# Gathering expert rows of x2 over its norm, with scale and shift applied behind the transposes, low parts on VectorE and an earlier routing of tiles 3 to 5

## The chip, the cores and the metric

The kernel runs on one core of a Trainium2 chip. The metric is the device time of one execution in microseconds, as the median of several runs. The profile is of one further execution. Its engines are TensorE (PE in the rows, with PEld for its weight loads), VectorE (DVE), ScalarE (ACT), GpSimd (POOL) and SyncE (SP), which issues most DMAs; an issue row has the engine's name with a q behind it.

## The reference

One layer with 1024 tokens of 1024 columns, and 256 context tokens. A mixer of gated linear attention and 2-D pooling ends in an output projection and a gated residual; behind it stands a mixture of 32 experts, two for each token. Cut to the part that the change touches:

```
x  = x + gt_a * (concat(o, pooled) @ w_out)                 # x2 in the kernel
h2 = rmsnorm(x, norm2_g) * (1 + sc_m) + sh_m                # norm2_g, sc_m, sh_m: one value a column
pg = softmax(h2 @ w_rg);  group = top 1 of 4
le = softmax of the 8 logits (h2 @ w_re) of that group;  experts = top 2
x  = x + gt_m * sum over the two experts of weight * (silu(a) * u) @ w_e_out,   a, u = h2 @ w_e_in
return rmsnorm(x, final_norm_g)
```

All arithmetic is f32. TensorE's products of f32 data are made of three passes with a high part (`hh`, `woh`) and a low part (`hl`, `wol`), the rest of a value less its high part. The products of the experts are done in one pass of f32.

## The kernel before, in words

**The mixer** (about 0 to 428 us) works on eight tiles of 128 tokens. A stretch at about 305 us opens its last part: `router_cols` transposes the 24 x 128 tile `rows` (shift, scale and gain of the second norm, for the router's weights `wr`), `pool_mix` makes 16 products of the pooled channels (L900), their evictions on ScalarE give the pooled half of `mix`, and the loop over the tiles (`n`, called the qp loop below) computes scores, masks them into `am`, and projects the first 512 columns of the output. Its loads go out on SyncE; `csl` is a table of constants for the routing. At `n == 6` the qp loop loads `shm` and `scm`, the shift and scale as rows of 1024 columns on all partitions, and VectorE multiplies the second norm's gain, loaded in two pieces `n2b`, into `scm` (L1056). This part ends at 428.

**The out1 loop** (428 to 495 us) makes the other 512 columns for the eight tiles, in an order that is written by hand for TensorE and VectorE; the other engines' order follows from it. A tile has 24 products of 128 x 512, three for each of eight pieces of the inner dimension, `tokproj(..., range(3))` and `range(3, 8)`. For a tile: `out_proj` makes the high part on ScalarE and the low part on GpSimd (L889; on VectorE for tile 0), `out1_x2` adds the residual in two operations on VectorE (L1302, L1303) and ScalarE sums the squares, `out1_rstd` gives `rst`, one over the norm, `logit1` transposes x2 for the router and `logit1_mm` multiplies it, `out1_bias` and an operation behind the logit products (L1334) give the logits `lga`. `out1_h2` makes the rows that the experts read: x2 times `rst` times `scm` on VectorE (L1323), plus `shm` on GpSimd (L1324), for tile 7 on ScalarE and GpSimd (L1320, L1321). The row goes to `h_d` in DRAM.

**The routing** works on three groups of tiles, A (0 to 2), B (3 to 5) and C (6, 7). For each group `route(a, b)` is a generator with three stages and a rest, all on VectorE: stage 1 chooses the expert group (L1111 to L1130, where L1099 repeats a small operation for each tile), stages 2 and 3 the two experts (to `ohb`, L1150), the rest their weights. Then TensorE counts tokens for each expert (`counts`, L1187), `place` gives each token its place, and `tables` adds up lists of tokens on TensorE (L1238, L1247). `idx`, the list for the gather, needs all three groups.

**The experts** (519 to about 784 us) run in blocks of up to 128 gathered tokens. GpSimd gathers rows of `h_d` into `hall`; `Block.rows` transposes a block in two halves of four transposes (L1644), ScalarE evicts the first half (L1650), VectorE the second (L1648), and the products with the experts' weights follow. Weights are loaded ahead into every slab of SBUF that has become free.

Of the kernel before, what the change touches and what calls it, by code (L numbers as in the profile page):

```python
# [14 lines left out]
OP = mybir.AluOpType  # L15
# [119 lines left out]
def hybrid_layer(ctx, tc, x, c, ctx_in, c_ctx, w_ada, b_ada, norm1_g, w_in, w_decay, b_decay, gla_norm_g,  # L135
# [44 lines left out]
    ones_r = early.tile([P, 32], F32, name="ones_r")  # L180
    ccol = early.tile([P, 8], F32, name="ccol")
# [670 lines left out]
    gta, shm, scm = hslab[0:3]  # L852
# [39 lines left out]
    with tc.tile_pool(name="qp", bufs=2) as qp:  # L892
        wbs = qp.tile([P, 36], F32, name="wbs", bufs=1)
        onef = qp.tile([P, P], F32, name="onef", bufs=1)
        gp.memset(onef, 1.0)

# [8 lines left out]
        def router_cols():  # L905

            pt = bank(6, 4, 5)
            te.transpose(pt[:, 0:24], rows, ident[:24, :24])
            col = qp.tile([P, 24], F32, name="col", bufs=1)
            ve.tensor_copy(col, pt[:, 0:24])  # L910
            ve.scalar_tensor_tensor(col[:, 8:16], col[:, 8:16], 1.0, col[:, 16:24], op0=OP.add, op1=OP.mult)
# [119 lines left out]
        with tc.manual_schedule(engines={mybir.EngineType.PE}):  # L1031
# [7 lines left out]
            for n in range(NT + 6):  # L1039
# [9 lines left out]
                if n == 6:  # L1049
                    sc.dma_start(shm, row_bcast(mod_d[D:2 * D], D))  # L1050
                    sc.dma_start(scm, row_bcast(mod_d[2 * D:3 * D], D))
                    for b in range(2):
                        ns = slice(b * 512, (b + 1) * 512)
                        n2b = qp.tile([P, 512], F32, name="xr")
                        sc.dma_start(n2b, row_bcast(norm2_g[0, ns], 512))
                        ve.scalar_tensor_tensor(scm[:, ns], scm[:, ns], 1.0, n2b, op0=OP.add, op1=OP.mult)  # L1056
# [235 lines left out]
    def out1_in(i):  # L1292
# [4 lines left out]
        po1[i], h1[i] = out_proj(i, wo2)  # L1297
# [17 lines left out]
    def out1_h2(i):  # L1315
        h2 = x2b[i % 3]
        for src, b in ((h2[:, 0:512], 0), (x1[i], 1)):
            dst, bs = h2[:, b * 512:(b + 1) * 512], slice(b * 512, (b + 1) * 512)
            if i == NT - 1:
                sc.activation(dst, src, AF.Copy, scale=rst[:, i:i + 1])  # L1320
                gp.tensor_tensor(dst, dst, scm[:, bs], OP.mult)  # L1321
            else:
                ve.scalar_tensor_tensor(dst, src, rst[:, i:i + 1], scm[:, bs], op0=OP.mult, op1=OP.mult)  # L1323
            gp.tensor_tensor(dst, dst, shm[:, bs], OP.add)  # L1324
        sy.dma_start(h2_d[i * P:(i + 1) * P], h2)
# [10 lines left out]
    with tc.manual_schedule(engines={mybir.EngineType.PE, mybir.EngineType.DVE}):  # L1336
        out1_in(0)
        for f in wo2_steps:
            f()
        rA, rB, rC = route(0, 3), route(3, 6), route(6, 8)  # L1340
        for n in range(NT):
            if n + 1 < NT:
                out1_in(n + 1)
            tokproj(po1[n], h1[n], wo2, range(3))
            if n:
                logit1(n - 1)
            tokproj(po1[n], h1[n], wo2, range(3, 8))
# [595 lines left out]
```

## Time and profile before

| | |
|---|---|
| median of 3 runs | 836.11 us (835.97 to 840.07) |
| the profiled execution | 842.28 us, its span 840.4 us, granted clock 0.937 |
| TensorE busy | 745.4 us, 89% of the span |
| VectorE busy | 432.0 us, 51% |
| ScalarE busy | 276.7 us, 33% |
| GpSimd busy | 208.7 us, 25% |
| read and written in DRAM | 179.81 and 29.63 MB, 249 GB/s over the span |

Busy shares are means over stages that differ. The granted clock is TensorE's, as a share of its full 2.4 GHz; a stretch with mean 0.79 has parts at either level. The profiled execution is 6.2 us longer than the median. Rows of the profile give the start, the duration, the engine, the line, the operation, what it writes and reads, and how often; in brackets the idle time of the engine before it and what ended that.

### The profile page before, as it was taken

What the parts mean: (1) busy time and instruction counts of PE and PEld (TensorE: products, weight loads), DVE (VectorE), ACT (ScalarE), POOL (GpSimd) and SP (SyncE); (2) the same over time, 40 slices, a digit from 0 to 9 for tenths busy, and PEclk for the clock granted to TensorE, in tenths of its full rate; (3) what the DMA queues carried; (4) which work ended last, traced back from release to release, by engine and by line L of the source; (5) the groups of instructions that cost most, each with busy time, mean ns of one, the idle gap of its engine ahead of it and who ended that gap; (6) DMA issues with size and microseconds to landing.
All of it is one profiled execution on the core that took longest, in us unless ns stands there. A gap on an engine that the chain in (4) does not pass through costs nothing. (4 is left out here: it accounts for less than half of the span.)

```text
span 840.4 us, 11818 instructions
## 1 busy us (share of the span) xinstructions
PE 745.4 (89%) x4106; PEld 502.2 (60%) x4106; DVE 432.0 (51%) x884; ACT 276.7 (33%) x526; POOL 208.7 (25%) x193
## 2 busy tenths in 40 slices
PE   4998999999999997879989575999999999989573
PEld 3676788788898966768878462434444433323232
DVE  4448856366776796654456877144123212212136
ACT  4777442345445564433433222201100101001023
POOL 2224100000001113344148544022222321222113
PEclk9899999989999998999999785999998999989788
DMA  9975875352531357554467658899999999999765
GB/s 326 290 274 181 276 236 184 120 161 90 182 133 50 135 158 282 188 180 162 136 226 257 218 213 287 305 374 347 349 393 361 338 305 336 396 344 381 241 227 201
DMA packets 78189, 206.80 MB, mean 246 GB/s; under 512 B 12460, under 2 KB 24864, under 8 KB 78129
## 3 DMA queue, kind: packets, MB, share of 16 engines
q1 hardware_dynamic: 70816, 185.45, 62.1%
q0 software_dynamic: 6560, 18.48, 9.0%
q10 hardware_dynamic: 752, 2.11, 0.7%
q8 instruction: 33, 0.54, 0.3%
q14 instruction: 28, 0.22, 0.1%
HBM read 179.81 MB, written 29.63 MB: 249 GB/s over the span
## 5 line engine op out<-in xcount | busy, mean ns | idle before, releaser
L1701 POOL DMA_INDIRECT x_d<-y,idx x26 | 38.4, 1477 | 138.0 <-DMA x_d<-y,idx 78.9
L1688 DVE SCALAR_TENSOR_TENSOR y<-bank,wtab,gtm 128x512 f32<-128x512 f32 (+1 forms) x40 | 29.7, 750 | 61.5 <-PE bank L1683 31.2
L1648 DVE COPY hh<-bank 128x512 f32<-128x512 f32 (+1 forms) x20 | 13.5, 675 | 79.2 <-PE bank L1644 79.0
L272 PE MATMUL bank<-woh,hh 128*128 128x512 f32 x124 | 52.8, 426 | 0.0
L273 PE MATMUL bank<-wol,hh 128*128 128x512 f32 x124 | 50.2, 405 | 0.8 <-DVE wol L200 0.8
L1674 ACT ACTIVATE gT<-bank 128x256 f32<-128x256 f32 (+1 forms) x20 | 7.4, 377 | 129.8 <-PE bank L1672 129.8
L274 PE MATMUL bank<-woh,hl 128*128 128x512 f32 x124 | 50.0, 403 | 0.1
L272 PE MATMUL bank<-wkh,hh 128*128 128x288 f32 (+1 forms) x144 | 42.9, 298 | 0.0
L1623 POOL DMA_INDIRECT hall<-h_d,idx x28 | 27.8, 994 | 60.1 <-PE bank L1644 52.0
L274 PE MATMUL bank<-wkh,hl 128*128 128x288 f32 (+1 forms) x144 | 42.0, 292 | 0.1
L273 PE MATMUL bank<-wkl,hh 128*128 128x288 f32 (+1 forms) x144 | 41.9, 291 | 0.0
L1659 PE MATMUL bank<-hall,hh 128*32 128x512 f32 (+4 forms) x156 | 40.9, 611 | 0.0
L200 POOL TENSOR_TENSOR wkl<-wraw,wkh 128x512 fp32r<-128x512 f32 x4 | 6.2, 1547 | 135.0 <-ACT wkh L199 135.0
L200 DVE TENSOR_TENSOR hl<-hall,hh 128x1024 fp32r<-128x1024 f32 x26 | 31.5, 1220 | 13.8 <-ACT hh L199 12.9
L1659 PE MATMUL bank<-mix,hh 128*64 128x512 f32 (+3 forms) x132 | 38.1, 600 | 0.0
L1659 PE MATMUL bank<-dS,hh 128*32 128x512 f32 (+4 forms) x88 | 37.0, 638 | 0.0
L199 ACT ACTIVATE hh<-hall 128x1024 fp32r<-128x1024 f32 x26 | 27.4, 1054 | 26.4 <-PE bank L273 22.2
L1666 DVE TENSOR_TENSOR ga<-ga,bank 128x256 f32<-128x256 f32 (+1 forms) x20 | 8.4, 421 | 48.5 <-ACT ga L1665 48.5
L272 PE MATMUL bank<-wvh,hh 128*128 128x512 f32 x80 | 32.2, 402 | 0.0
L273 PE MATMUL bank<-wvl,hh 128*128 128x512 f32 x80 | 32.0, 400 | 0.0
L274 PE MATMUL bank<-wvh,hl 128*128 128x512 f32 x80 | 31.8, 397 | 0.0
L1644 PEld LDWEIGHTS bank<-ident,hall 128*128 128x128 f32 (+1 forms) x160 | 22.7, 211 | 13.6 <-issue 11.9
(470 smaller groups left out, 1954.6 us busy)
## 6 DMA issues: line engine op xcount, KB each, us to landing
hall<-in_w_expert_in_dram SPq DMA_DIRECT2D x25, 512.0 KB
mix<-in_w_expert_in_dram SPq DMA_DIRECT2D x25, 512.0 KB
wat<-in_w_ada_dram SPq DMA_DIRECT2D x24, 512.0 KB
dS<-in_w_expert_in_dram SPq DMA_DIRECT2D x18, 512.0 KB
wraw<-in_w_ada_dram SPq DMA_DIRECT2D x16, 512.0 KB
wol<-in_w_expert_in_dram SPq DMA_DIRECT2D x14, 512.0 KB
woh<-in_w_expert_in_dram SPq DMA_DIRECT2D x13, 512.0 KB
wraw<-in_w_in_dram SPq DMA_DIRECT2D x12, 512.0 KB
```

The source lines that it names most:

```text
L199: sc.activation(hi, src, AF.Copy)
L200: en.tensor_tensor(lo, src, hi.bitcast(F32), OP.subtract)
L272: te.matmul(dst, lhsT=ah[k], rhs=bh[k], start=(k == ends[0]), stop=False)
L273: te.matmul(dst, lhsT=ah[k], rhs=bl[k], start=False, stop=False)
L274: te.matmul(dst, lhsT=al[k], rhs=bh[k], start=False, stop=(k == ends[1]))
L1623: gp.indirect_dma_start(out=self.xg[q], out_offset=None, in_=h2_d, in_offset=ix, bounds_check=D - 1, oob_is_err=False)
L1644: te.transpose(pt[:, j * m:(j + 1) * m], self.xg[:, k // 2 * 256 + k % 2:(k // 2 + 1) * 256:2], ident[0:m, 0:m])
L1648: ve.tensor_copy(self.xT[:, 4:8], pt)
L1659: te.matmul(self.ph[q], lhsT=self.xT[:, k, q], rhs=w[:, j * 512:(j + 1) * 512], start=(k == 0), stop=(k == 7))
L1666: ve.tensor_tensor(ga, ga, self.ph[0:m, 256:512], OP.mult)
L1688: ve.scalar_tensor_tensor(y[:, ns], py[n][0:m], self.wt, gtm[0:m, ns], op0=OP.mult, op1=OP.mult)
L1701: gp.indirect_dma_start(out=x2_d, out_offset=ix, in_=y[q], in_offset=None, bounds_check=D - 1, oob_is_err=False, compute_op=OP.add)
```

## The change

The rows that go to `h_d` are now x2 times `rst` alone, made by ScalarE in two operations (`out1_rows`); `shm` and `scm`, with their loads and L1056, are gone. Scale and shift are applied per column instead, where a block's columns lie on partitions: `Block.rows` evicts each 128 x 128 transpose apart, with a scale and a shift from `mcol`, four operations on ScalarE and four on VectorE a block. `mcol` comes from a 12 x 256 tile `rows4`, loaded by three DMAs on SyncE and transposed in `router_cols`. The low parts of the out1 loop are VectorE's (`out1_lo`), one tile ahead. In the loop, the sums `out1_x2` of a tile now stand behind all its products, `logit1_mm` behind six of the eight pieces, and group B is chosen, counted and placed within tile 7's products, its tables behind them.

```diff
-    gta, shm, scm = hslab[0:3]
+    gta = hslab[0]
...
+        rows4 = qp.tile([12, 2 * P], F32, name="rows4", bufs=1)
+        sy.dma_start(rows4[0:4], mod_d[D:2 * D].rearrange("(k p) -> k p", p=2 * P))
+        sy.dma_start(rows4[4:8], mod_d[2 * D:3 * D].rearrange("(k p) -> k p", p=2 * P))
+        sy.dma_start(rows4[8:12], norm2_g.rearrange("b (k p) -> (b k) p", p=2 * P))
...
             te.transpose(pt[:, 0:24], rows, ident[:24, :24])
+            for t in range(2):
+                te.transpose(pt[:, 24 + 12 * t:36 + 12 * t], rows4[:, t::2], ident[:12, :12])
             col = qp.tile([P, 24], F32, name="col", bufs=1)
             ve.tensor_copy(col, pt[:, 0:24])
+            col4 = qp.tile([P, 24], F32, name="col4", bufs=1)
+            ve.tensor_copy(col4, pt[:, 24:48])
+            for t in range(2):
+                c = col4[:, 12 * t:12 * t + 12]
+                ve.tensor_copy(mcol[:, 0, t::2], c[:, 0:4])
+                ve.scalar_tensor_tensor(mcol[:, 1, t::2], c[:, 4:8], 1.0, c[:, 8:12], op0=OP.add, op1=OP.mult)
...
-                if n == 6:
-                    sc.dma_start(shm, row_bcast(mod_d[D:2 * D], D))
-                    sc.dma_start(scm, row_bcast(mod_d[2 * D:3 * D], D))
-                    for b in range(2):
-                        ns = slice(b * 512, (b + 1) * 512)
-                        n2b = qp.tile([P, 512], F32, name="xr")
-                        sc.dma_start(n2b, row_bcast(norm2_g[0, ns], 512))
-                        ve.scalar_tensor_tensor(scm[:, ns], scm[:, ns], 1.0, n2b, op0=OP.add, op1=OP.mult)
...
-        po1[i], h1[i] = out_proj(i, wo2)
+        h1[i] = [wst.tile([P, 8, P], F32R, name=name, bufs=2) for name in ("hh", "hl")]
+        sc.activation(h1[i][0], mix(i), AF.Copy)
+        po1[i] = bank(0, 2)
+
+    def out1_lo(i):
+        hh, hl = h1[i]
+        ve.tensor_tensor(hl, mix(i), hh.bitcast(F32), OP.subtract)
...
-    def out1_h2(i):
+    def out1_rows(i):
+
         h2 = x2b[i % 3]
         for src, b in ((h2[:, 0:512], 0), (x1[i], 1)):
-            dst, bs = h2[:, b * 512:(b + 1) * 512], slice(b * 512, (b + 1) * 512)
-            if i == NT - 1:
-                sc.activation(dst, src, AF.Copy, scale=rst[:, i:i + 1])
-                gp.tensor_tensor(dst, dst, scm[:, bs], OP.mult)
-            else:
-                ve.scalar_tensor_tensor(dst, src, rst[:, i:i + 1], scm[:, bs], op0=OP.mult, op1=OP.mult)
-            gp.tensor_tensor(dst, dst, shm[:, bs], OP.add)
+            sc.activation(h2[:, b * 512:(b + 1) * 512], src, AF.Copy, scale=rst[:, i:i + 1])
         sy.dma_start(h2_d[i * P:(i + 1) * P], h2)
...
             tokproj(po1[n], h1[n], wo2, range(3))
+            if n + 1 < NT:
+                out1_lo(n + 1)
             if n:
                 logit1(n - 1)
-            tokproj(po1[n], h1[n], wo2, range(3, 8))
-            if n:
                 out1_bias(n - 1)
-                out1_h2(n - 1)
+                out1_rows(n - 1)
...
+            tokproj(po1[n], h1[n], wo2, range(3, 6))
             if n:
                 logit1_mm(n - 1)
-            out1_rstd(n)
+            if n == 3:
+                stage(rA)
+            if n == 4:
+                stage(rA)
...
             if n == 7:
-                stage(rB)
+                pcum = counts(3, 6)
+                SB = places_of(3, 6)
+                VB = values(3, 6)
+                for _ in place(3, 6, pcum, SB):
+                    pass
+            tokproj(po1[n], h1[n], wo2, range(6, 8))
+            out1_x2(n)
+            out1_rstd(n)
...
-                pt = pt.rearrange("p (j t) -> p j t", j=4)
-                if b:
-                    ve.tensor_copy(self.xT[:, 4:8], pt)
-                else:
-                    sc.activation(self.xT[:, 0:4], pt, AF.Copy)
+                for j in range(4):
+                    k = 4 * b + j
+                    dst, src = self.xT[:, k], pt[:, j * m:(j + 1) * m]
+                    shift, scale = (mcol[:, a, k:k + 1] for a in range(2))
+                    if b:
+                        ve.tensor_scalar(dst, src, scale, shift, op0=OP.mult, op1=OP.add)
+                    else:
+                        sc.activation(dst, src, AF.Identity, scale=scale, bias=shift)
```

Three places of the program's order follow; line numbers are those of the kernel that the rows are from.

**TensorE at the start of the mixer's last part, before.** The last products of the mixer's first part (high and low parts of weights, L273 and L274), the transposes of `rows`, and then `pool_mix`:

```order
L273 MATMUL bank_2911<-wkl,hh 128x256
L274 MATMUL bank_2911<-wkh,hl 128x256
L908 MATMUL bank_3016<-ident,rows 128x24
L900 MATMUL bank_3026<-mix_1159,wpg 128x512
L900 MATMUL bank_3027<-mix_1159,wpg 128x512
L900 MATMUL bank_3028<-mix_1159,wpg 128x512
```

**The same place of the change.** `rows_3005` is the tile `rows4`:

```order
L275 MATMUL bank_2912<-wkl,hh 128x256
L276 MATMUL bank_2912<-wkh,hl 128x256
L914 MATMUL bank_3021<-ident,rows 128x24
L916 MATMUL bank_3021<-ident,rows_3005 128x12 x2
L906 MATMUL bank_3039<-mix_1160,wpg 128x512
L906 MATMUL bank_3040<-mix_1160,wpg 128x512
L906 MATMUL bank_3041<-mix_1160,wpg 128x512
```

The two transposes of `rows4` have come between the transposes of `rows` and the products of `pool_mix`. On SyncE's queue the three loads of `rows4` stand directly behind the load of `csl` and ahead of the loads of `vb`, `gs` and `w_out`.

**VectorE where group A's stage 1 stands, before.** From the bias of tile 3 in the loop's turn `n == 4`, over the scaled rows and stage 1 (`gm` to `top`), to the sums of tile 4:

```order
L1313 SCALAR_TENSOR_TENSOR lga<-lga,rst,bias 128x36
L1323 SCALAR_TENSOR_TENSOR x2b_3998<-x2b_3998,rst,hall 128x512
L1323 SCALAR_TENSOR_TENSOR x2b_3998<-xr,rst,hall 128x512
L1111 TENSOR_REDUCE gm<-lga 128x3
L1099 SCALAR_TENSOR_TENSOR G<-lga,gm,csl 128x4 x3
L1117 TENSOR_REDUCE mn<-G 128x3
L1119 TENSOR_TENSOR G<-csl,mn 128x12
L1122 TENSOR_TENSOR gsel<-lga,G 128x96
L1126 TENSOR_REDUCE s_4318<-gsel 128x24
L1130 MAX top<-s_4318 128x8 x3
L1302 TENSOR_TENSOR x2b_3999<-bank_4211,hall 128x512
L1303 TENSOR_TENSOR xr<-x2b_3999,xr 128x512
```

**The same of the change,** in turn `n == 3`, from the low part of tile 4 (`hl`, L1309) over the logits of tile 2 and stage 1 to the sums of tile 3:

```order
L1309 TENSOR_TENSOR hl<-mix_1160,hh 128x1024
L1325 SCALAR_TENSOR_TENSOR lga<-lga,rst,bias 128x36
L1341 SCALAR_TENSOR_TENSOR lga<-bank_4242,rst,lga 128x36
L1117 TENSOR_REDUCE gm<-lga 128x3
L1105 SCALAR_TENSOR_TENSOR G<-lga,gm,csl 128x4 x3
L1123 TENSOR_REDUCE mn<-G 128x3
L1125 TENSOR_TENSOR G<-csl,mn 128x12
L1128 TENSOR_TENSOR gsel<-lga,G 128x96
L1132 TENSOR_REDUCE s_4259<-gsel 128x24
L1136 MAX top<-s_4259 128x8 x3
L1314 TENSOR_TENSOR x2b_4003<-bank_4155,hall 128x512
L1315 TENSOR_TENSOR xr<-x2b_4003,xr 128x512
```

The two scalings (L1323) have gone, a low part has come in their place, and stage 1 stands one tile earlier, behind the logits of tile 2.

**VectorE behind the loop, before.** From the logits of tile 6 over tile 7's norm and group B's second and third stage to `ohb` and the logits of tile 7 (L1334, last row):

```order
L1334 SCALAR_TENSOR_TENSOR lga<-bank_4596,rst,lga 128x36
L1309 TENSOR_TENSOR rst<-rst,ss_2997 128x1
L195 TENSOR_SCALAR rst<-rst 128x1
L1099 SCALAR_TENSOR_TENSOR O<-s_4562,top,csl 128x8 x6
L1135 TENSOR_REDUCE mn<-O 128x3
L1138 SCALAR_TENSOR_TENSOR O<-O,mn 128x8 x3
L1140 TENSOR_REDUCE mn<-O 128x3
L1313 SCALAR_TENSOR_TENSOR lga<-lga,rst,bias 128x36
L1143 TENSOR_TENSOR O<-csl,mn 128x3x8 x2
L1146 TENSOR_TENSOR ohall<-G,O 128x3x32 x2
L1150 TENSOR_TENSOR ohb<-ohall 128x96
L1334 SCALAR_TENSOR_TENSOR lga<-bank_4630,rst,lga 128x36
```

**The same of the change,** from tile 7's norm over its bias and group B's weights to its logits (L1341) and group C's stage 1:

```order
L1321 TENSOR_TENSOR rst<-rst,ss_2998 128x1
L197 TENSOR_SCALAR rst<-rst 128x1
L1183 TENSOR_REDUCE tot_f<-ohb 128x32
L1325 SCALAR_TENSOR_TENSOR lga<-lga,rst,bias 128x36
L1159 TENSOR_TENSOR eg<-lga,gm 128x12
L1161 TENSOR_TENSOR e_4665<-top 128x3
L1166 TENSOR_REDUCE den<-eg 128x3
L1168 SCALAR_TENSOR_TENSOR den<-e_4665,den 128x3
L1170 RECIPROCAL wgt<-den 128x3
L1172 TENSOR_TENSOR wgt<-wgt,e_4665 128x3
L1341 SCALAR_TENSOR_TENSOR lga<-bank_4674,rst,lga 128x36
L1117 TENSOR_REDUCE gm<-lga 128x2
```

Group B's choice no longer stands ahead of tile 7's logits; its weights do.

## Rows read from the trace of the kernel before

**Rows 1.** Two stretches: busy us (instructions) of PE, PEld, DVE, ACT, POOL, clock, DMA, GB/s.

```profile
462.00:495.00 33.00, 22.87 (x97) 18.76 (x97) 25.67 (x67) 6.76 (x18) 18.25 (x20) 0.79 0.63 221
...
560.00:640.00 80.00, 77.91 (x367) 34.18 (x364) 31.31 (x109) 7.73 (x17) 20.28 (x17) 0.97 1.03 366
```
**Rows 2.** TensorE in the out1 loop, in order of time.

```profile
438.24 0.40 PE L274 MATMUL bank<-woh,hl 128*128 128x512 f32 x1
...
445.09 0.40 PE L274 MATMUL bank<-woh,hl 128*128 128x512 f32 x1
...
467.85 1.08 PE L874 MATMUL bank<-ident,xr 128*128 128x128 f32 x4 [5.70 <-DVE xr L1303]
...
477.87 0.24 PE L1187 MATMUL bank<-ohb,tri 128*128 128x96 bf16 x1 [4.43 <-DVE ohb L1150]
...
480.73 0.63 PE L274 MATMUL bank<-woh,hl 128*128 128x512 f32 x1
```
**Rows 3.** TensorE behind the loop, until the experts' first transposes, in order of time.

```profile
494.70 0.39 PE L274 MATMUL bank<-woh,hl 128*128 128x512 f32 x1
494.93 0.68 PE L1238 MATMUL bank<-V,S 128*128 128x96 bf16 x12
...
500.33 1.92 PE L881 MATMUL bank<-wr,xT 128*128 128x36 f32 x8 [0.75 <-ACT xT L1330]
...
519.42 1.99 PE L1644 MATMUL bank<-ident,hall 128*128 128x128 f32 x8 [0.63 <-DMA hall<-h_d,idx]
```
**Rows 4.** VectorE in the loop and behind it, in order of time.

```profile
460.41 4.59 DVE L1099 SCALAR_TENSOR_TENSOR G<-lga,gm,csl 128x4 f32<-128x4 f32 x3
...
497.66 0.69 DVE L1303 TENSOR_TENSOR xr<-x2b,xr 128x512 f32<-128x512 f32 x1
...
506.20 0.24 DVE L1334 SCALAR_TENSOR_TENSOR lga<-bank,rst,lga 128x36 f32<-128x36 f32 x1
...
507.08 0.34 DVE L1099 SCALAR_TENSOR_TENSOR G<-lga,gm,csl 128x4 f32<-128x4 f32 x2
```
**Rows 5.** Groups of GpSimd's instructions between 429 and 519.4 us.

```profile
L1324 POOL TENSOR_TENSOR x2b<-x2b,hall 128x512 f32<-128x512 f32 x16 | 24.3, 1534 | 8.3 <-DVE x2b L1323 8.1
L889 POOL TENSOR_TENSOR hl<-mix,hh 128x1024 fp32r<-128x1024 f32 x6 | 14.7, 2447 | 7.3 <-ACT hh L888 7.3
```
**Rows 6.** TensorE and VectorE at the second norm's gain, in order of time.

```profile
366.99 0.66 PE L948 MATMUL bank<-ident,kb 128*128 128x128 f32 x4 [1.49 <-ACT mix L985]
...
368.77 0.69 DVE L1056 SCALAR_TENSOR_TENSOR hall<-hall,xr 128x512 f32<-128x512 f32 x1 [3.57 <-DMA xr<-in_norm_g_dram]
...
369.05 1.12 PE L874 MATMUL bank<-ident,x2h 128*128 128x128 f32 x4 [0.59 <-ACT qbT L950]
```
**Rows 7.** All engines from 304 us on, in order of time.

```profile
305.24 7.13 PE L900 MATMUL bank<-mix,wpg 128*128 128x512 f32 x16
...
306.22 2.83 SPq L863 DMA_DIRECT2D csl<-in_const_a_dram  x1
...
314.47 0.38 SPq L251 DMA_DIRECT2D wraw<-in_w_out_dram  x1
...
319.61 1.06 ACT L199 ACTIVATE woh<-wraw 128x1024 fp32r<-128x1024 f32 x1 [2.20 <-DMA wraw<-in_w_out_dram]
...
325.23 0.77 PE L972 MATMUL bank<-hall,am 128*128 128x128 f32 x2 [4.53 <-DVE am L964]
```
**Rows 8.** Groups of instructions of the whole span, from the page.

```profile
L1648 DVE COPY hh<-bank 128x512 f32<-128x512 f32 (+1 forms) x20 | 13.5, 675 | 79.2 <-PE bank L1644 79.0
...
L1674 ACT ACTIVATE gT<-bank 128x256 f32<-128x256 f32 (+1 forms) x20 | 7.4, 377 | 129.8 <-PE bank L1672 129.8
...
L200 DVE TENSOR_TENSOR hl<-hall,hh 128x1024 fp32r<-128x1024 f32 x26 | 31.5, 1220 | 13.8 <-ACT hh L199 12.9
```
**Rows 9.** TensorE in a block of the experts, in order of time.

```profile
556.12 1.23 PE L1644 MATMUL bank<-ident,hall 128*128 128x128 f32 x8
...
562.99 1.46 PE L1659 MATMUL bank<-woh,hh 128*64 128x512 f32 x6
```

More of the change, by code (lines that the diff above doesn't have):

```diff
@@ L180, in hybrid_layer @@
     ones_r = early.tile([P, 32], F32, name="ones_r")
+    mcol = early.tile([P, 2, 8], F32, name="mcol")
     ccol = early.tile([P, 8], F32, name="ccol")
@@ L1337, in hybrid_layer @@
         out1_in(0)
+        out1_lo(0)
         for f in wo2_steps:
@@ L1353, in hybrid_layer @@
             if n == 5:
+                pcum = counts(0, 3)
+                stage(rA)
                 for _ in rA:
@@ L1357, in hybrid_layer @@
                 stage(rB)
-            out1_x2(n)
-            if n == 7:
-                tables(tsum, VA, SA, 0, 3, stop=False)
-                tables(wsum, VA, SA, 3, 6, stop=False)
-                pair_tables(fsum, VA, SA, start=False, stop=False)
-            if n == 5:
-                pcum = counts(0, 3)
+                stage(rB)
+            tokproj(po1[n], h1[n], wo2, range(3, 6))
             if n:
                 logit1_mm(n - 1)
-            out1_rstd(n)
+            if n == 3:
+                stage(rA)
+            if n == 4:
+                stage(rA)
             if n == 5:
@@ L1374, in hybrid_layer @@
                 weights(0, 3, VA)
-            if n == 7:
-                stage(rB)
-        i = NT - 1
-        logit1(i)
-        out1_bias(i)
-        stage(rB)
-        logit1_mm(i)
-        pcum = counts(3, 6)
-        total(6)
-        SB = places_of(3, 6)
-        VB = values(3, 6)
-        pB = place(3, 6, pcum, SB)
-        stage(rC, pB)
-        for _ in pB:
-            pass
+            if n == 6:
+                stage(rB)
+                tables(tsum, VA, SA, 0, 3, stop=False)
+                tables(wsum, VA, SA, 3, 6, stop=False)
+                pair_tables(fsum, VA, SA, start=False, stop=False)
+            if n == 7:
+                pcum = counts(3, 6)
[6 more added lines that the diff above has]
+            out1_rstd(n)
+        i = NT - 1
         tables(tsum, VB, SB, 0, 3, start=False, stop=False)
         pair_tables(fsum, VB, SB, start=False)
+        logit1(i)
+        total(6)
+        out1_bias(i)
+        for _ in rB:
+            pass
+        logit1_mm(i)
         tab = rt.tile([P, 3, E], F32, name="tab_ab")
@@ L1395, in hybrid_layer @@
         sc.activation(tabf, fsum.rearrange("p (a e) -> p a e", e=NP), AF.Copy)
-        out1_h2(i)
-        stage(rB)
-        stage(rC, rB)
-        stage(rC, rB)
-        for _ in rB:
-            pass
+        out1_rows(i)
+        stage(rC)
+        stage(rC)
+        stage(rC)
         weights(3, 6, VB)
```

## The prediction

> **What bounds the kernel now.** I read the stretches first, then TensorE's own order of time where a stretch is not full, then the engine that TensorE waited for there. In the experts TensorE is busy for 77.91 of 80 us at a granted clock of 0.97, and the DMA engines are full too [rows 1]: an earlier start carries over to the end, but nothing inside that phase is cheap. The slack lies before it. In the later half of the loop over the eight tiles (the output projection's second 512 columns) TensorE is busy for 22.87 of 33 us at a clock of 0.79 [rows 1], and in the routing behind the loop it mostly stands. The loop's own rows show what is lost: an undisturbed tile takes 445.09 - 438.24 = 6.85 us from its last product to the next tile's, while the six tiles from 438.24 to 494.70 take 56.46 us, 15.4 more than six times 6.85 [rows 2, 3]. Two idle stretches, 5.70 and 4.43 us, both ended by VectorE, make 10.1 of that, and after each the products run for a while at the lower of TensorE's two levels, 1.2 GHz (0.63 us a product against 0.40) [rows 2]. VectorE was late because three routing operations took 4.59 us; two of the same kind took 0.34 us once GpSimd was quiet [rows 4]. What GpSimd did beside them is its shift of 128x512 (1534 ns, 16 times) and its low parts (2447 ns) [rows 5].
>
> **The change, term by term.** *The loop.* GpSimd loses both groups of rows 5. The low parts go to VectorE at 1220 ns each [rows 8], VectorE's scaling of the rows goes to ScalarE, so VectorE's load per tile barely changes, and it no longer works beside GpSimd. The routing operations should then take the 0.17 us of the undisturbed pair, and a stage some 2.1 us (12 operations, an estimate from that row). I walked VectorE's new order through six tiles. Routing stage 1 ahead of tile 3's sum delays it by 0.8 us; nine products, 2.06 us, stand before the transposes that need it, so TensorE loses some 0.25 there, 0.35 a tile later. The group's placing and weights stand ahead of tile 5's sum: about 1.95 us late, of which 1.25 remains, and the tables of group A (24 short products, 0.68 us for the first twelve [rows 3]; 1.2 us in all is an estimate, with the counts) now run inside the loop. Group B's counts wait for its choice: 1.1. Together 0.25 + 0.35 + 2.45 + 1.1 = 4.15 instead of 15.4: **-11.2**. No idle here comes near the two that dropped the clock. Bounds: -15.4 if all goes, -6 if one of the two idles comes back.
>
> *The routing behind it.* From the last product (494.70) to the experts' first transposes (519.42) is 24.7 us. Tile 7's sum ended at 498.35, 3.65 behind that product, because a routing stage stood ahead of it [rows 4]; now group B's place operations do, which I put at 2.35 us with the sum itself (an estimate from VectorE's new order), so -1.3. From there to the logit correction at 506.20 were 7.85 us [rows 4], since that operation was queued behind group B's choice, although the logit products (500.33, 1.92 at the low level [rows 3]) were over at 502.25. Group B is now done earlier, so the correction runs some 0.2 us after them: 4.1, -3.75. Behind it group C's own operations no longer alternate with group B's: about -1. In sum **-6.1**; bounds -2 (VectorE as slow as before) and -9.
>
> *The columns of scale and shift.* Two transposes of the new 12-row tile stand on TensorE between the transposes of `rows` and the 16 products of the pool mixer, which began at 305.24 and need nothing of it [rows 7]. The three loads are issued behind `csl`, which held SP until 309.05; so they go out at about 309.2 to 310.3. Nothing shows such a load's landing; the nearest is w_out's, issued at 314.47 and waited for until ScalarE's high part at 319.61, 5.1 us for 512 KB [rows 7]. Far smaller loads may take half of that. I take 313 (bounds 311 and 315.5). TensorE thus stands for 7.7 us, and its first products behind it run at the low level, as at 480.73: some 2.3 more, 10 in all. Queued behind are the pool mixer, its evictions on ScalarE and all scores. Part is hidden: 4.53 us of idle at 325.23 were set by w_out's late split, not by TensorE, and the products behind it ran at the low level (0.77 for two) [rows 7]. The chain from the scores through the mask still needs about 2.8 of it (three operations of 512 columns, one of them over two tiles of SBUF and twice as long as the 675 ns of [rows 8], an estimate), so 1.7 are absorbed, and some 2.6 come back if the shorter idle keeps the clock up. Loss **+5**, bounds 0 and +9.
>
> *The row-wide scale and shift that go.* VectorE waited 3.57 us for a piece of the second norm's gain (368.77), ahead of work that TensorE needed: its idles of 1.49 and 0.59 us, and four transposes at 1.12 instead of 0.66 us, lie round it [rows 6]. That is 2.1 us of waiting and about 1.4 of low level: **-3.5**, bounds 0 and -6.
>
> *Eviction with scale and shift.* One eviction of 128x512 becomes four of 128x128, on both engines, for 20 blocks. From 377 ns for 256 columns and 675 ns for 512 [rows 8], 128 columns cost about 0.25 to 0.3 us, four 1.0 to 1.2, so +0.5 a block. In a running block the transposes at 556.12 are used by products at 562.99, 6.9 us later [rows 9]; the two evictions now take about 2.5 of it instead of 1.3. Cost nothing, except in the first block, which has no other work: **+0.5**. Without the cover it would be 20 x 0.5 = 10 us.
>
> The Trainium skill, VectorE: DVE Perf Modes, "The TRN2 errata", speaks against this edit: many small tiles pay a latency per instruction, and it advises 512 elements and more. By its table (120 cycles plus the columns, out of PSUM) an estimate for four is 1.03 us against 0.66, +0.4 a block, 7.5 us over 20 if each block showed it; the rows have the same fixed part, and the cover decides.
>
> Sum: -11.2 - 6.1 + 5 - 3.5 + 0.5 = **-15.3**. The profiled execution took 842.28 us (span 840.4), so it would take 827.0; the median of the runs is 6.2 lower, and the same difference gives 836.1 - 15.3 = **821**.
>
> **Rivals.** *The experts give it back.* With the DMA engines at 1.03 of their time [rows 1] weights may arrive no earlier than now, and TensorE would wait for them, or the small evictions show. Against it: before 495 the DMA engines are at 0.63, with room to run ahead. If half is lost, 828; if the evictions show in full, 831. Chance 0.17.
>
> *More than forecast.* The three loads land by 311 or w_out's split hides the wait, and the gain of the second norm's load is whole: 5 to 8 us more, 813 to 816. Chance 0.12.
>
> *VectorE becomes the bound of the loop.* It takes 1.2 us of low part in each tile, in front of the sums that TensorE's transposes need, and the routing on top. If a tile's period rises to 6.85 + 2 in all six, 12 of the 11.2 won are lost: 833. Against it: VectorE was busy for 25.67 of 33 us, but with operations stretched beside GpSimd [rows 1, 4]. Chance 0.07.
>
> *Slower: TensorE stands at the new transposes.* This is one wait with a price that grows with the landing: each us past 313 costs one. From about 328 the other gains are used up, from 332 the kernel is slower by over 0.5%, some 840. That needs 22 us from issue to landing, four times the longest of rows 7; the loads might also be held on SP for a tile that must first be free. `csl` itself was held for 2.83 us there, so SP does wait at this place. Chance 0.08.
>
> The Trainium skill, DMA: Bandwidth & Descriptors, gives a small transfer a fixed cost of about 2.0 us. By it the landing would be 312.3, and the estimate of the loss 0.7 lower; no row of before shows such a load alone.
>
> **How the numbers follow.** The forecast holds 0.56, with its own range of 815 to 827: the bounds of its terms are independent, so not all lie on one side. With the larger gain and most of the loss in the experts, 811 to 832 leaves some 2 in 10 out. A measurement here can tell about 0.5%, 4.2 us, from no change. Faster: 0.56 + 0.12 + 0.13 of the experts' rival, 0.81. Same: 0.04 of that, 0.04 of VectorE's and 0.02 of the landing's, 0.10. Slower: 0.03 + 0.06 = 0.09.
>
> **What would show it.** Tile to tile in the loop near 6.85 us with no idle over 2 us and the clock at full; the routing operations at 0.17 us; from the last product of the loop to the experts' transposes about 18.6 us instead of 24.7; an idle of some 7 us on TensorE at 305, ended by a DMA; no wait for the second norm's gain; four evictions of about 0.27 us with no TensorE wait behind them. I am wrong if a wait for VectorE recurs at each tile, if TensorE waits for weights after 560 where it did not, or if the idle at 305 is far from 7 us.

## The result, and the profile after

The changed kernel took 824.71 us in the median of 4 runs (822.77 to 829.43), against 838.09 us before (835.97 to 841.27, 4 runs): a ratio of 0.986, 95% interval 0.982 to 0.990, so 8 to 15 us less. Its profiled execution took 825.45 us, with a span of 823.6.

The two profiled executions differ by 16.8 us of span, but 4.31 of these lie ahead of the change: the transposes of `rows` stand at 305.07, just ahead of the pool mixer [rows 7], and now at 300.76. In eleven more profiles, whose work up to there is the same, they stand between 301.5 and 309.3. So the stages are compared from that point on, each by itself. In the table, *mask* is the first product that waits for the masked scores `am`, *wait* TensorE's wait for w_out's low part ahead of the out1 loop, *loop* the time from the product that ended this wait to tile 7's last product, *routing* from there to the experts' first transposes, *experts* from there to the end of the span. All are differences of starts of TensorE's rows; *mask to wait* leaves the wait out. Two of the rows of before that they go by:

```profile
305.07 0.24 PE L908 MATMUL bank<-ident,rows 24*128 24x24 f32 x1
...
429.12 0.50 PE L273 MATMUL bank<-wol,hh 128*128 128x512 f32 x1 [0.76 <-DVE wol L200]
```

| us | rows to mask | mask to wait | wait | loop | routing | experts |
|---|---|---|---|---|---|---|
| before | 20.16 | 103.13 | 0.76 | 65.58 | 24.72 | 320.98 |
| after | 26.80 | 95.35 | 2.27 | 55.46 | 21.00 | 321.96 |
| difference | +6.64 | -7.78 | +1.51 | -10.12 | -3.72 | +0.98 |

The sum is -12.5, near the 13.4 of the medians. The start of the mixer's last part, in order of time on TensorE:

```profile
300.76 0.24 PE L914 MATMUL bank<-ident,rows 24*128 24x24 f32 x1
307.42 0.38 PE L916 MATMUL bank<-ident,rows 12*128 12x12 f32 x2 [6.42 <-DMA rows<-in_norm_g_dram]
307.73 9.72 PE L906 MATMUL bank<-mix,wpg 128*128 128x512 f32 x16
...
327.56 0.46 PE L986 MATMUL bank<-hall,am 128*128 128x128 f32 x2 [2.52 <-DVE am L978]
```
The wait ahead of the pool mixer is there, 6.42 us, and a DMA ended it; the mixer's 16 products took 9.72 us instead of 7.13 [rows 7]. The mask's wait shrank from 4.53 [rows 7] to 2.52, and the products behind it ran at full clock: the first two take 0.46 us instead of 0.77 [rows 7].

The loop and the routing behind it, on TensorE:

```profile
425.18 0.63 PE L275 MATMUL bank<-wol,hh 128*128 128x512 f32 x1 [2.27 <-DVE wol L202]
425.61 0.63 PE L276 MATMUL bank<-woh,hl 128*128 128x512 f32 x1
...
434.65 0.39 PE L276 MATMUL bank<-woh,hl 128*128 128x512 f32 x1
...
467.40 0.63 PE L876 MATMUL bank<-ident,xr 128*128 128x128 f32 x4 [2.06 <-DVE xr L1315]
...
480.64 0.40 PE L276 MATMUL bank<-woh,hl 128*128 128x512 f32 x1
...
491.03 0.21 PE L1193 MATMUL bank<-ohb,tri 128*128 128x64 bf16 x1 [5.38 <-DVE ohb L1156]
...
501.64 1.98 PE L1656 MATMUL bank<-ident,hall 128*128 128x128 f32 x8 [3.32 <-DMA hall<-h_d,idx]
```
And VectorE, with the table operation that leads to the first of these waits, routing stage 1 of group A, the sums of tiles 5 and 7, the logits of tile 7 and the list `idx`:

```profile
423.80 0.20 DVE L1611 TENSOR_SCALAR tab<-csl 128x28 int32<-128x28 f32 x1 [3.13 <-DMA x_d<-x2h]
423.90 1.22 DVE L202 TENSOR_TENSOR wol<-wraw,woh 128x1024 fp32r<-128x1024 f32 x1
...
447.85 0.49 DVE L1105 SCALAR_TENSOR_TENSOR G<-lga,gm,csl 128x4 f32<-128x4 f32 x3
...
466.57 0.69 DVE L1315 TENSOR_TENSOR xr<-x2b,xr 128x512 f32<-128x512 f32 x1
...
482.07 0.69 DVE L1315 TENSOR_TENSOR xr<-x2b,xr 128x512 f32<-128x512 f32 x1
...
486.29 0.25 DVE L1341 SCALAR_TENSOR_TENSOR lga<-bank,rst,lga 128x36 f32<-128x36 f32 x1
...
493.46 0.16 DVE L1427 SCALAR_TENSOR_TENSOR idx<-bank,tab 128x4 int32<-128x4 f32 x1
```
The three routing operations of stage 1 take 0.49 us (4.59 before [rows 4]). The longest idle in the loop is 2.06 us, for tile 5's sum at 466.57, which stands behind group A's placing. New is the wait of 2.27 us at 425.18, with products at 0.63 us behind it: VectorE's table operation `tab` waits 3.13 us for the store of a tile of the mixer, and the last split of w_out stands behind it. The experts' evictions, from the page:

```profile
L1663 DVE TENSOR_SCALAR hh<-bank,mcol 128x128 f32<-128x128 f32 (+1 forms) x80 | 27.0, 399 | 69.5 <-PE bank L1656 69.3
...
L1665 ACT ACTIVATE hh<-bank,mcol 128x128 f32<-128x128 f32 (+1 forms) x80 | 29.9, 454 | 45.5 <-PE bank L1656 43.1
```

### The profile page after: what moved, and what is told of

Read it like the earlier page. It is cut to its first block, busy times and chain, and to the rows that moved or that the text cites. A ratio compares the mean times of both kernels' runs of the same rounds, so it can differ in the third digit from the quotient of the medians.

```text
span 823.6 us, 11914 instructions
## 1 busy us (share of the span) xinstructions
PE 732.7 (89%) x4108; PEld 492.0 (60%) x4108; DVE 428.2 (52%) x940; ACT 304.0 (37%) x600; POOL 169.3 (21%) x168
## 5 line engine op out<-in xcount | busy, mean ns | idle before, releaser
L1663 DVE TENSOR_SCALAR hh<-bank,mcol 128x128 f32<-128x128 f32 (+1 forms) x80 | 27.0, 399 | 69.5 <-PE bank L1656 69.3
L274 PE MATMUL bank<-woh,hh 128*128 128x512 f32 x124 | 51.5, 415 | 0.0
L1665 ACT ACTIVATE hh<-bank,mcol 128x128 f32<-128x128 f32 (+1 forms) x80 | 29.9, 454 | 45.5 <-PE bank L1656 43.1
L274 PE MATMUL bank<-wkh,hh 128*128 128x288 f32 (+1 forms) x144 | 42.7, 297 | 0.0
L274 PE MATMUL bank<-wvh,hh 128*128 128x512 f32 x80 | 31.4, 392 | 0.0
```

What stands on the lines that cost most here:

```text
L274: te.matmul(dst, lhsT=ah[k], rhs=bh[k], start=(k == ends[0]), stop=False)
L1663: ve.tensor_scalar(dst, src, scale, shift, op0=OP.mult, op1=OP.add)
L1665: sc.activation(dst, src, AF.Identity, scale=scale, bias=shift)
```

## The experiments

Each ratio is the kernel's median over that of the kernel before, with its 95% interval; the stages stand in one table at the end of this section.

**The order of before, GpSimd quiet.** The kernel before, its order kept, with its loads and all of the mixer as they were; it leaves out the scale and shift of the rows.

```diff
-        (gp if i and w is not wo else ve).tensor_tensor(hl, src, hh.bitcast(F32), OP.subtract)
+        ve.tensor_tensor(hl, src, hh.bitcast(F32), OP.subtract)
...
-            gp.tensor_tensor(dst, dst, shm[:, bs], OP.add)
+            sc.activation(h2[:, b * 512:(b + 1) * 512], src, AF.Copy, scale=rst[:, i:i + 1])
```

> The kernel before, in its own order, with nothing for GpSimd to do in the loop: low parts on VectorE, rows made by ScalarE as x2 times the norm. It leaves out the scale and shift of the rows. Theory (GpSimd beside VectorE stretches the routing operations): the three operations at 460.41 fall from 4.59 us to about 0.6, both TensorE idles fall under 2 us, the stretch from the w_out wait to the last product falls from 65.6 us to about 57, the routing behind it by some 3 us; 827 in all. Rival (the written order is what counts): the idles keep 3 us or more each, the stretch stays at 63 to 66 us, 835 to 838.

819.16 us, ratio 0.977 (0.974 to 0.980). The theory holds, and the effect is larger than it said: the loop takes 48.98 us, 6.5 less than in the changed kernel, and the routing falls to 20.55 with its order unchanged. On TensorE two waits are left in the loop:

```profile
431.27 0.50 PE L273 MATMUL bank<-wol,hh 128*128 128x512 f32 x1 [0.57 <-DVE wol L200]
...
435.08 0.63 PE L874 MATMUL bank<-ident,xr 128*128 128x128 f32 x4 [0.34 <-issue]
```
VectorE in the same stretch, groups of instructions:

```profile
L1303 DVE TENSOR_TENSOR xr<-x2b,xr 128x512 f32<-128x512 f32 x8 | 5.5, 692 | 1.0 <-DMA xr<-in_x_dram 0.8
L1302 DVE TENSOR_TENSOR x2b<-bank,hall 128x512 f32<-128x512 f32 x8 | 5.5, 691 | 8.3 <-PE bank L274 7.8 <-issue 0.4
...
L1099 DVE SCALAR_TENSOR_TENSOR G<-lga,gm,csl 128x4 f32<-128x4 f32 x8 | 1.3, 219 | 0.1
```
The first and the last of them in the kernel before, from 415 to 500 us:

```profile
L1303 DVE TENSOR_TENSOR xr<-x2b,xr 128x512 f32<-128x512 f32 x8 | 9.2, 1146 | 0.8 <-DMA xr<-in_x_dram 0.6
L1099 DVE SCALAR_TENSOR_TENSOR G<-lga,gm,csl 128x4 f32<-128x4 f32 x6 | 7.0, 1221 | 0.1
```
L1303 has two operands in SBUF, and takes 692 ns where it took 1146 beside GpSimd; L1302 reads PSUM and one operand in SBUF, and takes 691 ns here and 685 before. The routing operation L1099 falls from 1221 ns to 219.

How an operation is stretched shows in the kernel before, where the three of 4.59 us [rows 4] stand one by one beside GpSimd's, in order of time:

```profile
459.71 1.74 POOL L1324 TENSOR_TENSOR x2b<-x2b,hall 128x512 f32<-128x512 f32 x1 [1.03 <-DVE x2b L1323]
460.41 1.06 DVE L1099 SCALAR_TENSOR_TENSOR G<-lga,gm,csl 128x4 f32<-128x4 f32 x1
461.39 1.31 DVE L1099 SCALAR_TENSOR_TENSOR G<-lga,gm,csl 128x4 f32<-128x4 f32 x1
461.41 1.28 POOL L1324 TENSOR_TENSOR x2b<-x2b,hall 128x512 f32<-128x512 f32 x1
462.62 2.37 DVE L1099 SCALAR_TENSOR_TENSOR G<-lga,gm,csl 128x4 f32<-128x4 f32 x1
462.64 2.34 POOL L889 TENSOR_TENSOR hl<-mix,hh 128x1024 fp32r<-128x1024 f32 x1
```
Each of the three ends within 0.02 us of the operation of GpSimd beside it: at 461.47, 462.70 and 464.99 against 461.45, 462.69 and 464.98. Each lasts until GpSimd's operation is over, however small it is itself.

**The new order, GpSimd busy.** The changed kernel with the low parts of tiles 1 to 7 on GpSimd and a row of zeros added to the rows, so GpSimd has its old work back and the order is new.

```diff
+        (gp if i else ve).tensor_tensor(hl, mix(i), hh.bitcast(F32), OP.subtract)
...
+            gp.tensor_tensor(dst, dst, zrow[:, b * 512:(b + 1) * 512], OP.add)
```

> The changed kernel with GpSimd busy again: it makes the low parts of tiles 1 to 7 and adds a row of zeros to each half of the rows, as many and as large operations as before the change. Theory (GpSimd beside VectorE): routing operations of 1 us each and more, TensorE idles of 4 us and more in two or three tiles, the stretch of the loop 61 to 65 us instead of 55.5, 831 to 834 in all. Rival (the order): the stretch stays within 1.5 us of 55.5, 824 to 827.

836.08 us, ratio 0.999 (0.996 to 1.001): the whole gain is gone, and the loop, 67.30 us, is longer than before. VectorE:

```profile
448.66 4.56 DVE L1107 SCALAR_TENSOR_TENSOR G<-lga,gm,csl 128x4 f32<-128x4 f32 x3
...
473.55 2.57 DVE L1317 TENSOR_TENSOR xr<-x2b,xr 128x512 f32<-128x512 f32 x1
```
TensorE's two longest waits in its loop:

```profile
456.06 0.63 PE L876 MATMUL bank<-ident,xr 128*128 128x128 f32 x4 [4.41 <-DVE xr L1317]
...
476.27 1.09 PE L876 MATMUL bank<-ident,xr 128*128 128x128 f32 x4 [4.59 <-DVE xr L1317]
```
The order of the change, without a quiet GpSimd, wins nothing in the loop. Behind the loop it does: the routing takes 19.12 us here, 5.6 less than before. The gather's landing varies from kernel to kernel (see the last experiment), so the list `idx` is the better mark. The last product of the loop and `idx`, first with the old order and GpSimd quiet, then with the new order and GpSimd busy:

```profile
480.25 0.39 PE L274 MATMUL bank<-woh,hl 128*128 128x512 f32 x1
...
493.78 0.16 DVE L1409 SCALAR_TENSOR_TENSOR idx<-bank,tab 128x4 int32<-128x4 f32 x1
```
```profile
493.46 0.40 PE L276 MATMUL bank<-woh,hl 128*128 128x512 f32 x1
...
507.68 0.16 DVE L1431 SCALAR_TENSOR_TENSOR idx<-bank,tab 128x4 int32<-128x4 f32 x1
```
From the one to the end of the other are 13.7 and 14.4 us. In the kernel before it was 19.7, in the change 13.0: either half of the change alone gives most of what is won up to `idx`.

**One half of GpSimd's work at a time,** in the kernel before: first the low parts to VectorE, then, by itself, the rows to ScalarE (scale and shift left out). The edits are the two of the first experiment, one each.

> The kernel before with its low parts on VectorE and nothing else changed, so GpSimd keeps the 16 additions of the shift (24.3 of its 39 us). Theory (VectorE is stretched for as long as GpSimd works beside it): the three routing operations still take 2 us or more in one group, the loop 58 to 62 us, 829 to 834 in all. Rival (the low parts, 2.4 us at a time, are what hits the routing): no idle over 1 us, the loop 50 to 53, 821 to 825.

> The kernel before with the rows made by ScalarE as x2 times the norm; it leaves out their scale and shift. The low parts stay on GpSimd. Theory (time beside GpSimd): 15 of 39 us of GpSimd's work are left, the loop 53 to 58 us, 825 to 829. Rival (the low parts are what hits): idles of 3 us and more stay, the loop 60 or more, 832 to 836.

The low parts alone: 832.41 us, ratio 0.995 (0.992 to 0.999), loop 58.37, routing unchanged at 24.83. The rows alone: 818.95 us, ratio 0.981 (0.975 to 0.987), loop 52.78, routing 19.68. So most of it is the rows, which take 24.3 us off GpSimd and two operations a tile off VectorE; the second gained more than was expected. That VectorE's lighter load is not what counts is shown by the experiment ahead of this one: there VectorE has neither these two operations nor the low parts of tiles 1 to 7, and the loop takes 67.30 us. In the first, the routing operations are still stretched:

```profile
458.24 2.43 DVE L1099 SCALAR_TENSOR_TENSOR G<-lga,gm,csl 128x4 f32<-128x4 f32 x3
...
467.59 3.00 DVE L1099 SCALAR_TENSOR_TENSOR O<-s,top,csl 128x8 f32<-128x8 f32 x6
```

**The new order against the old one, with everything else of the change.** First the transposes of `rows4` were put behind the pool mixer and the router's bias (the next experiment's kernel), then in that kernel the loop and the routing were put back into the order of before; of the edit, the products and the places of bias and rows:

```diff
-            tokproj(po1[n], h1[n], wo2, range(3, 6))
+            tokproj(po1[n], h1[n], wo2, range(3, 8))
+            if n:
+                out1_bias(n - 1)
+                out1_rows(n - 1)
...
-            tokproj(po1[n], h1[n], wo2, range(6, 8))
             out1_x2(n)
```

> The kernel of rows4_behind with the loop and the routing behind it in the order of before; scale and shift stay in the evictions, the low parts on VectorE. Theory (with GpSimd quiet the new order only adds waits and group work to the loop): from the w_out wait to the last product 49 to 50 us instead of 55.4, the routing behind it longer by 1 us or less, 814 to 815.5 in all. Rival (the new order pays behind the loop): the loop wins 5 us and the routing loses 4 or more, 819 to 820.5.

815.45 us, ratio 0.970 (0.966 to 0.974): 4.9 us less than with the new order, the loop 49.99 instead of 55.38, the routing 21.62 instead of 19.74. The wait ahead of its loop, on TensorE; no other wait for VectorE follows up to the last product:

```profile
424.11 0.79 PE L275 MATMUL bank<-wol,hh 128*128 128x512 f32 x1 [1.89 <-DVE wol L202]
```
The new order costs 5.4 us in the loop and gives back some 2 behind it; the two intervals, 0.966 to 0.974 and 0.976 to 0.981, do not meet. This kernel beats both: 3% under the kernel before, and about 9 us under the changed one (815.45 against 824.71).

**The transposes behind the pool mixer.**

```diff
-            for t in range(2):
-                te.transpose(pt[:, 24 + 12 * t:36 + 12 * t], rows4[:, t::2], ident[:12, :12])
...
             ve.tensor_copy(bias, pb[:, 0:36])
+            pt = bank(6, 4, 5)
+            for t in range(2):
+                te.transpose(pt[:, 24 + 12 * t:36 + 12 * t], rows4[:, t::2], ident[:12, :12])
```

> The changed kernel with the two transposes of the 12-row tile behind the pool mixer and the router's bias. Theory (TensorE's wait at 301 to 307 is paid for, less what the mask's chain hid): the idle of 6.42 us goes, 3 to 4 us less, 821. Rival (what follows waits for w_out's split and the mask anyway): the idle moves to the mask's chain at about 321, with the clock at half behind it, 824 to 825.5.

820.32 us, ratio 0.979 (0.976 to 0.981), 4.4 less than the changed kernel. TensorE:

```profile
307.34 0.24 PE L914 MATMUL bank<-ident,rows 24*128 24x24 f32 x1
307.50 7.13 PE L906 MATMUL bank<-mix,wpg 128*128 128x512 f32 x16
...
315.95 0.40 PE L929 MATMUL bank<-ident,rows 12*128 12x12 f32 x2
...
326.77 0.74 PE L987 MATMUL bank<-hall,am 128*128 128x128 f32 x2 [2.87 <-DVE am L979]
```
From `rows` to the mask 19.43 us instead of 26.80. A wait of 2.87 for the mask stays, this time with products at the lower level behind it (0.74 for the first two), which takes 1.6 of the 7.4 back in the next stage. The wait of [rows 7] is thus a cost of the change of 4 to 6 us, as its term said.

**The 12-row tile in memory that was there anyway.** The tiles of the routing and the experts lie where they did not touch the mixer's pool; 1.1 KB more of that pool was suspected to reach under them.

```diff
-        rows4 = qp.tile([12, 2 * P], F32, name="rows4", bufs=1)
+        wb = qp.tile([P, 8, 36], F32, name="wb", bufs=1)
+        rows4 = wb.rearrange("p k n -> p (k n)")[0:12, 0:2 * P]
...
-            col4 = qp.tile([P, 24], F32, name="col4", bufs=1)
+            col4 = wbs[:, 0:24]
```

> The changed kernel with the 12-row tile in the memory of wb and its columns in that of wbs, so that the qp pool is as large as before the change. Theory (the 1.1 KB more of the pool reaches under the tables that are made at the start of the last part, so these wait for the pool's last store, and VectorE's last split of w_out waits behind them): the table operation goes back from 423.8 to about 316, TensorE's wait at the start of the loop from 2.27 to about 0.8 us with the clock staying at full, 3 us less: 821.7. Rival (w_out's own load sets that wait): the table moves, the wait stays over 1.8 us, 824 to 825.

824.92 us, ratio 0.986 (0.982 to 0.990): no shorter. Yet the mechanism is there. VectorE makes the table early, without a wait, here on VectorE in order of time:

```profile
328.53 0.20 DVE L1611 TENSOR_SCALAR tab<-csl 128x28 int32<-128x28 f32 x1
```

And TensorE waits 0.75 us ahead of the loop, with its products at full clock:

```profile
435.48 0.50 PE L275 MATMUL bank<-wol,hh 128*128 128x512 f32 x1 [0.75 <-DVE wol L202]
```

The stage from mask to wait took 98.39 us instead of 95.35. There the clock was 0.90 in the first 33 us behind the mask's wait of 2.53 us (a stretch's columns as in [rows 1]):

```profile
336.30:369.00 32.70, 29.32 (x211) 25.70 (x212) 20.22 (x31) 14.50 (x28) 11.48 (x9) 0.90 0.42 133
```

In the changed kernel, behind a wait of 2.52, it was 1.00:

```profile
327.56:360.00 32.44, 29.09 (x222) 25.18 (x223) 22.57 (x34) 15.60 (x29) 13.67 (x11) 1.00 0.48 155
```

Over the whole stage TensorE was busy for 93.03 us instead of 90.02, with 613 instructions in both. So this execution lost its 3 us to the clock; that the edit has no part in this is not shown. The runs (822.55 to 833.34) are too far apart to show a gain of that size: the two longest, 832.60 and 833.34, had a granted clock of 0.938 and 0.937, the other four 0.949 to 0.951.

**The table operation on GpSimd.** The pools as in the change; one operation moved.

```diff
-        ve.tensor_scalar(tab[:, :, 3], xnum, BIG, -NDB * BIG, op0=OP.mult, op1=OP.add)
+        gp.tensor_scalar(tab[:, :, 3], xnum, BIG, -NDB * BIG, op0=OP.mult, op1=OP.add)
```

> The changed kernel with the one table operation that stood ahead of VectorE's last split of w_out given to GpSimd; the pools stay as they are, so GpSimd's eight token operations stay late too. Theory: TensorE's wait at the start of the loop 0.8 us instead of 2.27, the clock stays at full there, the mixer's part stays short (95 us from the mask to that wait, not 98 as in rows4_in_wb); 3 us less, 821.7. Rival (the load of w_out sets the wait): 824 to 825.

> The kernel of old_order with the one table operation ahead of w_out's last split given to GpSimd. Theory: TensorE's wait at the start of the loop 0.8 us instead of 1.9, its products there at full clock, 1 to 2.5 us less: 813 to 814.5. Rival (as in tab_on_gpsimd, the lost time comes back at another place): 815 to 816.

In the changed kernel: 823.79 us, ratio 0.981 (0.979 to 0.984). In the kernel of the old order: 813.87 us, ratio 0.976 (0.971 to 0.981), and 0.970 (0.966 to 0.974) without it. Between those pairs the intervals overlap, so no gain is shown. TensorE in the first:

```profile
426.99 0.50 PE L275 MATMUL bank<-wol,hh 128*128 128x512 f32 x1 [0.76 <-DVE wol L202]
...
468.47 0.63 PE L876 MATMUL bank<-ident,xr 128*128 128x128 f32 x4 [1.94 <-DVE xr L1315]
...
469.29 0.63 PE L275 MATMUL bank<-wol,hh 128*128 128x512 f32 x1
```
The wait is 0.76 us and the products behind it run at full clock, but behind a wait of 1.94 in the loop they now run at 0.63. In the changed kernel it was the other way round, 2.27 with and 2.06 without a fall. The mask's wait, too, was 2.53 us with a fall here (0.77 us for the first two products), and 2.52 without in the changed kernel. The edit takes the wait away; what the clock does at the next wait decides whether anything is left of it.

**One eviction instead of four** (no scale and shift in the result; the four instructions of a half become the one of before).

```diff
-                for j in range(4):
...
-                        sc.activation(dst, src, AF.Identity, scale=scale, bias=shift)
+                pt = pt.rearrange("p (j t) -> p j t", j=4)
+                if b:
+                    ve.tensor_copy(self.xT[:, 4:8], pt)
+                else:
+                    sc.activation(self.xT[:, 0:4], pt, AF.Copy)
```

> The changed kernel with one eviction for each half block, without scale and shift (left out of the result). Theory (the four evictions are hidden, but for the first block): from the experts' first transposes to the end 0.5 to 1 us less, 824. Rival (they stand between transposes and products in most blocks): 4 us or more less, 820 or under.

824.17 us, ratio 0.982 (0.978 to 0.986). The medians of 824.17 and 824.71 cannot be told apart. The experts took 318.72 us, and 318.4 to 321.0 in the five profiles with one eviction, against 319.6 to 324.0 in the eight with four. The means, 319.3 and 322.0, speak for a cost of about 2.7 us, more than the theory allowed; the two ranges overlap and the kernels differ in other things too, so it stays open, and so does where it is lost: none of TensorE's longer waits names the evictions.

**The weights held behind the gather.** In the changed kernel the gather of the first block, issued at 493.91, was waited for until 501.64, 7.7 us; before it was 4.7 us. Seven loads of weights, 3.6 MB, are issued in the 7.3 us ahead of it (486.61 to 491.65), six such loads before the change.

```diff
+    for t in slabs[-7:]:
+        sc.activation(t[:, 0:1], cnt[:, 0:1], AF.Copy)
```

> The changed kernel with seven of the loads of experts' weights held until the list for the gather is made (a small write of ScalarE into their slabs). Theory (the first gather queues behind 3.6 MB of weights issued just ahead of it): from the gather's issue to the first transposes under 5.5 us instead of 7.7, and 2 to 3 us less, 822. Rival (the landing varies by itself, and the weights are needed): the gather is no faster or the weights are late in the first blocks, 825 to 829.

826.04 us, ratio 0.983 (0.980 to 0.986): no gain. The gather took 5.86 us (500.22 to 506.08) and the routing 19.14, 1.9 less, while the experts took 324.02, 2.1 more. But the run does not separate the two readings: the held loads are issued from 500.90 to 505.14, while the gather is under way:

```profile
500.90 0.33 SPq L1286 DMA_DIRECT2D woh<-in_w_expert_in_dram  x1
...
503.14 2.00 SPq L1286 DMA_DIRECT2D wol<-in_w_expert_in_dram  x4
```

The other twelve profiles say more. Where five or six loads of experts' weights are issued in the 8.6 us ahead of the gather, as before, it took 4.45 to 4.92 us (four profiles; one of these is the changed kernel with its 12-row tile in other memory); where seven to nine are, as in the change, 5.71 to 7.93 (eight profiles). That fits the theory that the gather queues behind them, but no run changed the number of loads and nothing else, so it is not shown.

The stages of all kernels:

| us | rows to mask | mask to wait | wait | loop | routing | experts |
|---|---|---|---|---|---|---|
| old order, GpSimd quiet | 21.32 | 102.41 | 0.57 | 48.98 | 20.55 | 318.40 |
| new order, GpSimd busy | 26.95 | 95.41 | 2.29 | 67.30 | 19.12 | 322.62 |
| low parts on VectorE | 20.86 | 105.52 | 0.77 | 58.37 | 24.83 | 319.28 |
| rows on ScalarE | 20.17 | 102.32 | 0.75 | 52.78 | 19.68 | 319.09 |
| transposes behind | 19.43 | 96.95 | 2.28 | 55.38 | 19.74 | 319.58 |
| the same, old order | 20.38 | 97.08 | 1.89 | 49.99 | 21.62 | 321.98 |
| the same, table on GpSimd | 19.56 | 95.27 | 0.76 | 49.70 | 21.89 | 322.88 |
| tile in other memory | 27.04 | 98.39 | 0.75 | 54.60 | 18.12 | 322.60 |
| table on GpSimd | 26.36 | 96.73 | 0.76 | 56.32 | 20.16 | 320.53 |
| one eviction | 26.08 | 97.01 | 1.93 | 55.42 | 19.87 | 318.72 |
| weights held | 25.86 | 96.86 | 2.27 | 55.42 | 19.14 | 324.02 |

## Why the prediction was right, and where it was not

The forecast was 821 us, 15.1 less; 13.4 less was measured, within the stated range of 811 to 832 and the likeliest case's own.

*The loop*: -11.2 was forecast for the six tiles from 438.24; the same six take 45.99 us instead of 56.46 (434.65 to 480.64), -10.5. The reason is shown: a quiet GpSimd alone brings the loop to 48.98, and a busy one alone takes the change's loop to 67.30. The terms for the new order fit too: 0.36 us at tile 3, 2.06 at tile 5 (1.25 forecast, beside 1.2 for tables and counts), 0.60 for group B's counts (1.1). The forecast did not ask what the old order would do with a quiet GpSimd: its loop is 5.4 us better.

*The routing*: -6.1 was forecast, -3.7 came. Up to `idx` it came out a little better than forecast (18.6 less the gather's 4.7 is 13.9): the sum of tile 7 ended 2.1 us behind its last product (2.35 forecast), the logits came 3.5 us later (4.1), and `idx` was done at 493.62, 13.0 us behind that product, 6.7 less than before. The step that failed is the last: the gather's landing was carried over unchanged, and took 7.7 us instead of 4.7. Why is not settled; the change issues seven loads of weights in the 7.3 us ahead of it, and with that many it was slow in other kernels too. The reason given, group B's earlier place, is only one of two: the new order beside a busy GpSimd comes to 14.4 us up to `idx`, the old order beside a quiet one to 13.7. Before, group B's choice stood ahead of tile 7's logits and was stretched as well; it is enough to take one of the two away.

*The columns*: the wait was forecast at 7.7 us and was 6.42, since the last of the loads landed 1.7 us behind its issue at 305.72, not 2.7. The products at the lower level cost 2.6 us (2.3 forecast), and 1.6 came back behind the mask's wait (2.6). The forecast's own parts, 7.7 and 2.3 less 1.7 and 2.6, add up to 5.7, not 5; taking the wait out gave 4.4 us. The Trainium skill (DMA: Bandwidth & Descriptors, section "Anatomy of one DMA — SWDGE (gpsimd) path") gives about 2.0 us as the fixed cost of a transfer, from a fit to transfers that GpSimd issues; for these, which SyncE issues, that was nearer to the 1.7 measured than my value.

*The second norm's loads*: mis-sized. -3.5 was forecast. The kernel with the transposes behind the pool mixer has, as the kernel before, products at the lower level behind the mask's wait; from mask to wait it takes 96.95 us, 6.2 less than before. In all kernels that kept these loads that stage took 102.3 to 105.5, in those without 95.3 to 98.4. So they were worth 5 to 6 us, at the end of the forecast's bounds.

*The evictions*: mis-sized. An eviction of 128 columns (112 in a quarter of them) with scale and shift takes 454 ns on ScalarE and 399 on VectorE, not 250 to 300; four of them 1.51 and 1.37 us in the first block, not 1.0 to 1.2. None of TensorE's longer waits names them, and the first block's products begin 1.91 us behind its transposes (501.64 to 503.55), as before (1.92). The experts lost 0.98 us here (0.5 forecast), within the spread between executions; the means of all profiles speak for 2.7, so that the cover holds in full is not shown.

*Not forecast*: the wait at the loop's start, 1.5 us and 1.6 at the lower level. It follows from the size of a pool, which the change made larger: with the new tile in memory that was there, the table operation went from 423.80 to 328.53 and the wait to 0.75.

That the sum came so near is in part luck. By the stages, the loop, the routing, the experts and the wait at the loop's start came out 5.5 us worse than forecast together, and the second norm's loads 2.7 better.

The rivals: VectorE did not become the bound, TensorE did not stand at 305 for longer than forecast, and the experts gave back 1 us, not half of the gain.

## What to carry to other kernels

Before an order is rewritten around an engine that is late, see whether its operations take as long as the same ones elsewhere in the trace: here three of them took 4.59 us instead of 0.49. Taking the load off the neighbour was the cure, and with that the old order was the better one. A value that is needed only 200 us later should not be fetched by an in-order engine at the head of its busiest stretch. And when a pool grows, look which tiles it now reaches under; the wait turns up somewhere else, on an engine that has nothing to do with the new tile.

## What the runs showed of the hardware

VectorE beside GpSimd: an operation of 128x512 with two operands in SBUF takes 692 ns with GpSimd quiet, and 1146 in the mean (2.57 us at worst in the new order, GpSimd busy) beside it, one with an operand in PSUM 684 to 692 in every kernel. Small operations suffer most: one of 128x4 took 1221 ns in the mean and takes 219, since in the rows it ended only when GpSimd's operation beside it did. It goes the other way as well: GpSimd's `rst` takes 0.55 us where VectorE has no low part beside it, and 1.47 (437.72 in the changed kernel) where it has. The Trainium skill says in GPSIMD Engine Reference, section "8. Key points", that GpSimd shares its SBUF interfaces with VectorE, with contention for VectorE's operations that have two inputs in SBUF; the runs agree.

The clock behind a wait of about 2 us: TensorE fell to 1.2 GHz behind waits of 2.27, 1.94, 2.87 and 2.53 us and stayed at 2.4 GHz behind others of 2.06 and 2.52. A fall cost 1.6 us at the loop's start, 2.6 in the pool mixer and 3.0 in the stage behind the mask's wait. That is as much as the smaller edits here are worth, and executions of one kernel differ by more.
